# Which engine waits for the last store: moving the closing semaphore wait of an add-and-GELU kernel from SyncE to ScalarE

## The chip, the cores and the metric

The kernel runs on one core of a Trainium2 chip. The metric is the device time of one execution in microseconds (us), as a median over runs. The **span** is the time from the start of the first of the program's own instructions to the end of the last; it comes from the profile. All runs below are in the fast state. In some executions, of the kernel before too, the span is 0.4 to 0.9 us longer than in most; medians are little touched by that, and where less than 0.1 us matters I compare the time minus the span of one profiled execution, to which the store's landing adds nothing. Times are on record to 0.01 us, so the third digit of such a difference is no evidence; means over all runs of a kernel are given below as a check.

Engines: PE is TensorE, DVE is VectorE, ACT is ScalarE, POOL is GpSimd, SP is SyncE.

## The reference

```python
def setup_inputs():
    batch, dim = 1024, 4096
    # x, y: float32 of [batch, dim]
def reference(x, y):
    z = x + y
    return (0.5 * z * (1 + np.tanh(np.sqrt(2 / np.pi) * (z + 0.044715 * z ** 3)))).astype(np.float32)
```

## The kernel before

Loads, adds (mostly on GpSimd), two passes on ScalarE, two on VectorE, and three stores, all issued by SyncE. The change concerns none of it, only the end. Without `wait_late` the program closes as the run `undo_late` below shows: SyncE waits 11.5 us for its stores, the four other engines have a semaphore record at 119.1 to 119.2 us, GpSimd clears the semaphores at 119.4 us (a record of 95 ns), and all five have one at 119.7 us. I call these the kernel's own closing barriers, with the clearing between them. `wait_late`, run on the finished program, takes the last store out of that first wait, leaves its semaphore out of the clearing, and puts the wait for it at the very end, so that barriers and clearing run under the last store (in the kernel before from 111.75 to 112.49 us, with the last count of the store at 118.744 us):

```python
def wait_late(nc):
    body, end = (b.instructions for b in nc.main_func.blocks[1:3])
    last = [i for i in body if isinstance(i, mybir.InstDMACopy)][-1]
    (sem,) = [u.id for u in last.sync_info.on_update]
    # ... (cut: finds the closing wait, the clearing and its range)
    (its,) = [w for w in waits if w.id == sem]
    end[0] = mybir.InstDrain(   # waits for all but the last store
        name=all_done.name, engine=all_done.engine, debug=all_done.debug, is_reset_sema=False,
        sync_info=mybir.SyncInfo(on_wait=[w for w in waits if w.id != sem], on_update=[]),
    )
    # ... (cut: clears the semaphores on both sides of sem)
    end.append(
        mybir.InstEventSemaphore(
            name=clear.name, engine=mybir.EngineType.SP, debug=clear.debug,
            sync_info=mybir.SyncInfo(
                on_wait=[its],
                on_update=[
                    mybir.SyncUpdate(
                        sync_type="semaphore", id=sem, ant_name=its.ant_name,
                        update_mode="sem-sub-imm", update_value=its.wait_value,
                    )
                ],
            ),
        )
    )
```

## Time and profile before

| | before |
|---|---|
| time, median of 3 runs | 120.35 us (120.22 to 120.42) |
| span of the profiled run | 118.8 us |
| time of the profiled run minus its span | 120.44 − 118.778 = 1.66 us |
| busiest compute engine | VectorE, 62% of the span |
| DMA queue | 98.8% of 16 engines' time |

The kernel is bound by its transfers. The row to look at is the last: 1.66 us of the time lie outside the program's own instructions, and the change acts there. No page of the profile shows that part. The trace does, through its record of semaphore updates, which goes on after the program's last instruction (the prediction below shows the page's lines and reads them). Semaphore 2 is named by none of the 172 instructions that the trace holds, and yet it is updated 18 times from 112.727 to 120.227 us, in two groups of nine. I call a group a **barrier of the runtime**, since no line of the kernel makes it. The name is mine. The trace also has 223 updates of other semaphores, one of each, 0.26 to 0.87 us after the span's end, most of them between the two groups, and the texts call them resets. The 1.45 us from the span's end to the last update are what the prediction calls the postamble. A **hop** here is the time from one update of semaphore 2 to the next.

### The profile page before, as it was taken

The page shows a single profiled execution, that of the slowest core. Times are in us where ns is not written, and L with a number is a line of the kernel's source. Part 1 is how long each engine was busy: PE and PEld are TensorE (multiplying, and loading weights), DVE is VectorE, ACT ScalarE, POOL GpSimd, SP SyncE. Part 2 cuts the span into 40 slices and gives each one's busy share as a digit, 9 for nine tenths or more (in the row PEclk, how much of TensorE's full clock was granted, in tenths as well). Part 3 has the DMA queues.
Part 4 walks back from the last instruction along what each step waited for, and adds up shares of the span by engine and source line. Part 5 has one row for each costly group of instructions (what it writes and reads, how often), then busy time and mean ns, then how long its engine had stood idle before and what let it go on. Part 6 is the DMA issues. An engine that isn't in the chain of part 4 may idle for free.

```text
span 118.8 us, 172 instructions
## 1 busy us (share of the span) xinstructions
DVE 73.7 (62%) x35; ACT 61.0 (51%) x34; POOL 69.6 (59%) x19
## 2 busy tenths in 40 slices
DVE  0000000635799995739999968999994999990000
ACT  5000000063888965197698647888839779810000
POOL 0000000699996099999959999959999990000000
DMA  7989898989999898989899898998899889999996
GB/s 243 463 386 497 353 530 353 508 375 475 408 419 463 375 508 353 519 364 508 375 430 452 386 497 353 519 541 353 353 596 463 353 353 441 441 441 441 389 406 265
DMA packets 1584, 50.33 MB, mean 424 GB/s; under 512 B 176, under 2 KB 176, under 8 KB 176
## 3 DMA queue, kind: packets, MB, share of 16 engines
q1 hardware_dynamic: 1584, 50.33, 98.8%
HBM read 33.55 MB, written 16.78 MB: 424 GB/s over the span
## 4 chain that ended last, share of the span: by engine, by line
DMA 51%; POOL 26%; POOLq 4%; DVE 4%; DVEq 2%; ACT 2%; issue 0%; SPq 0%
DMA y<-in_y_dram 51%; POOL z L152 26%; POOLq L230 4%; DVE w L163 2%; DVEq L230 2%; DVE z L175 2%; ACT w L157 2%; SPq L128 0%; POOLq L152 0%
## 5 line engine op out<-in xcount | busy, mean ns | idle before, releaser
L152 POOL TENSOR_TENSOR z<-z,y 128x2048 f32<-128x2048 f32 x15 | 69.4, 4658 | 28.3 <-DMA y<-in_y_dram 28.3
L157 ACT ACTIVATE w<-z 128x2048 f32<-128x2048 f32 x16 | 30.1, 1882 | 37.7 <-DVE z L152 21.5
L163 DVE SCALAR_TENSOR_TENSOR w<-w,z 128x2048 f32<-128x2048 f32 x16 | 36.7, 2296 | 11.3 <-ACT w L157 11.1
L175 DVE TENSOR_TENSOR z<-w,z 128x2048 f32<-128x2048 f32 (+1 forms) x17 | 35.9, 2155 | 0.0
L168 ACT ACTIVATE w<-w 128x2048 f32<-128x2048 f32 x16 | 29.7, 1855 | 4.4 <-DVE w L163 4.3
L152 DVE TENSOR_TENSOR z<-z,y 128x2048 f32<-128x2048 f32 x1 | 2.3, 2291 | 20.5 <-DMA y<-in_y_dram 20.5
L215 ACT ACT_TABLE_LOAD x1 | 1.3, 1283 | 1.3 <-PEq L247 1.3
L214 DVE MEMSET one<- 128x1 f32 x1 | 0.1, 59 | 1.3 <-PEq L247 1.3
L247 POOL MEMSET const-float32-0.0<- 128x1 f32 x1 | 0.1, 99 | 0.2 <-issue 0.2
L215 ACT ACTIVATE one<-one 128x1 f32<-128x1 f32 x1 | 0.2, 203 | 0.0
L247 POOL MEMSET const-bfloat16-1.0<- 128x1 bf16 x1 | 0.1, 101 | 0.0
L247 POOL MEMSET const-uint8-127<- 128x1 uint8 x1 | 0.1, 101 | 0.0
L247 POOL MEMSET const-float32-1.0<- 128x1 f32 x1 | 0.1, 98 | 0.0
## 6 DMA issues: line engine op xcount, KB each, us to landing
z<-in_x_dram SPq DMA_DIRECT2D x4, 4096.0 KB, 31.4
y<-in_y_dram SPq DMA_DIRECT2D x4, 4096.0 KB, 22.2
out_dram<-z SPq DMA_DIRECT2D x1, 5120.0 KB, 15.8
out_dram<-z SPq DMA_DIRECT2D x1, 3072.0 KB, 11.9
out_dram<-z SPq DMA_DIRECT2D x1, 22.0
```

Source lines behind the costliest of these rows:

```text
L152: eng.tensor_add(out=zt[:, a:b], in0=zt[:, a:b], in1=yt[s][:, o : o + b - a])
L157: nc.scalar.activation(out=wt[c], in_=zt[:, a:b], func=act.Square, scale=root)
L163: nc.vector.scalar_tensor_tensor(out=wt[c], in0=wt[c], scalar=c1, in1=zt[:, a:b], op0=alu.add, op1=alu.mult)
L168: nc.scalar.activation(out=wt[c], in_=wt[c], func=act.Sigmoid)
L175: ins = nc.vector.tensor_mul(out=zt[:, a + o : a + o + n], in0=wt[c][:, o : o + n], in1=zt[:, a + o : a + o + n],)
L214: nc.vector.memset(one, 0.0)
L215: nc.scalar.activation(out=one, in_=one, func=act.Sigmoid)
L230: tc.compile()
L247: nc = _bacc.Bacc("TRN2", target_bir_lowering=False, num_devices=1)
```

## The change

ScalarE is idle at the end; the change lets it hold the last wait, so that SyncE, which issued every transfer, is free 6.3 us earlier.

```diff
     end.append(
         mybir.InstEventSemaphore(
-            name=clear.name, engine=mybir.EngineType.SP, debug=clear.debug,
+            name=clear.name, engine=mybir.EngineType.Activation, debug=clear.debug,
             sync_info=mybir.SyncInfo(
                 on_wait=[its],
```

## The prediction

> **What bounds the kernel now.** I read the views in this order: the page, to see which resource is full; the wait view of SyncE's queue, to see who holds the end of the program; the records of the line that closes the kernel; and last the trace's semaphore updates after the final instruction, which no page prints. From the page:
>
> ```profile
> span 118.8 us, 172 instructions
> DVE 73.7 (62%) x35; ACT 61.0 (51%) x34; POOL 69.6 (59%) x19
> DVE  0000000635799995739999968999994999990000
> ACT  5000000063888965197698647888839779810000
> POOL 0000000699996099999959999959999990000000
> DMA  7989898989999898989899898998899889999996
> q1 hardware_dynamic: 1584, 50.33, 98.8%
> DMA 51%; POOL 26%; POOLq 4%; DVE 4%; DVEq 2%; ACT 2%; issue 0%; SPq 0%
> ```
>
> The reader is to see that no compute engine passes 62% of the span, while the packets of the one DMA queue fill 98.8% of the 16 DMA engines' time. The kernel is bound by moving 50.33 MB. In the last four slices all three compute rows are 0 and the DMA row is still 9, 9, 9, 6: the program ends with a store alone. The chain adds to about 90%, since it is followed back from the last instruction of a compute engine (a VectorE multiply that ends at 106.84 us), so it says nothing of the last 12 us, which is where the change lies. For these I took one stretch, 107 to 119 us, with the busy time of each engine:
>
> ```profile
> 107.00:119.00 12.00, 0.00 (x0) 0.00 (x0) 0.00 (x0) 1.00 0.86 371
> ```
>
> Compute is 0.00 us, DMA 0.86 busy at 371 GB/s. Then the waits of SyncE's queue, the four lines that bear on the end:
>
> ```profile
> SPq L230 <- SPq L230: 6.3, 1, 6.3
> SPq L230 <- DMA out_dram<-z: 4.2, 1, 4.2
> SPq L230 <- PEq L230: 0.6, 2, 0.5
> ```
>
> The columns are total us, times, longest. (The fourth is the issue of the last store at 106.86 us, in the timeline.) The 4.2 us are the wait for the stores before the last. The 6.3 us are the wait that the change moves: SyncE passes the kernel's own closing barrier at 112.43 us, then sits until the last store's count is full. The view names SyncE itself as releaser only because SyncE's subtraction is the last update of that semaphore. The records of the closing line give the instruction behind it:
>
> ```profile
> L230 SPq EVENT_SEMAPHORE  x7: 17/28/4226, 107.2 to 118.8; - x7
> L230 ACTq EVENT_SEMAPHORE  x2: 17/17/17, 111.9 to 112.4; - x2
> ```
>
> SyncE's seventh starts at 118.8 us and ends the span; ScalarE's last is at 112.4 us, so ScalarE has been idle for 6.3 us by then.
>
> [...] the 6.3 us wait has a record of 17 ns. [...] The trace shows 16 increments, from 118.260 to 118.744 us, and the subtraction at 118.778. [...] The trace shows such hops, nine updates of semaphore 2 a barrier, 23 to 47 ns apart where nothing holds them; [...] the last update of semaphore 2 is at 120.227 us, 1.45 us after the span ends.
>
> **The change part by part.** *Removed and added:* one semaphore instruction leaves SyncE's stream and the same one, same wait, same subtraction, joins the end of ScalarE's. The comparison of the two programs' streams says "the same" for all five engines (it lists no semaphore instructions), so loads, compute and stores do not move: 118.744 us, when the count fills, stays. Bandwidth and bytes stay.
>
> *The wake-up:* in the closing barrier at 112.4 us both engines wait for one semaphore; SyncE's record starts at 112.430, ScalarE's at 112.434, both 17 ns. I take +0.004 us. What follows: from SyncE's record (118.761) to its update of the runtime's barrier (118.918) are 157 ns. For ScalarE I take the same, since from the barrier record to the next drain both engines need 91 to 92 ns at 111.9 us.
>
> *The place in the runtime's barrier:* this is the term that I think matters. In the barrier after the kernel four updates come at 112.727, 112.761, 112.966 and 113.010 us, all engines but SyncE; then nothing until SyncE's at 118.918; then 118.962, 119.001, 119.035, 119.082. [...] all others have already handed up, and only four hops down are left, 44 + 39 + 34 + 47 = 164 ns. If ScalarE comes last, the hops up from ScalarE to SyncE must still be made. The second barrier, which nothing holds, shows the steps: 119.870, .904, .942, .986, 120.010, .108, .146, .181, .227, that is 34, 38, 44, 24, 98, 38, 35, 46 ns. ScalarE's place I infer: in the kernel's own barrier SyncE answers 34 ns after the release, ScalarE 45, VectorE 57; 11 and 23 ns over SyncE, and the second place answers in 34 ns and the fourth in 44 against SyncE's 24, so ScalarE is second and VectorE fourth. From the second place: up 38 + 44 + 24 = 106 ns, then down 98 + 38 + 35 + 46 = 217, together 323 ns. The 98 is more than the 44 of before because the fourth engine has only just made its own update, and its next comes 122 ns after that one. So 323 − 164 = +159 ns. [...]
>
> *Sum:* 0.004 + 0.159 = +0.16 us, 0.14% of 120.35. The run that was profiled took 120.44 us against a span of 118.78; the 1.66 us between fit the 1.45 us of postamble plus a little at the start, so I count the postamble as timed. 120.35 + 0.16 = **120.5 us**.
>
> **The rivals.** *Nothing at all:* the wait only changes its owner, and the count fills at 118.744 either way. It holds if the timing stops at the span's end [...]. For it: the runs of one kernel spread from 120.22 to 120.42, more than my term. It would give 120.35. *A small gain:* SyncE owns the queue of all the stores; set free at 112.45 us, it might do some end-of-program work of its own under the last store, a part of the 157 ns. Against it: the four engines that were free before got no further than one barrier update each, and that barrier opens only when the last comes. At most some 0.1 us, so 120.25. *A slower sequencer:* ScalarE, after a 6 us wait, might need more than 157 ns to reach the barrier. VectorE and TensorE are slower than SyncE in the closing barrier, ScalarE only by 4 to 11 ns. TensorE's answer, 57 ns over SyncE's, is the worst there, so at most +0.06, 120.57. *A different place:* if ScalarE were first, one hop of 34 ns more (+0.19); if fourth, only 24 + (98 − 44) = 78 ns (+0.08). Every place is later than SyncE's.
>
> **Range and chances.** The mechanism gives +0.08 to +0.25; the runs' spread is 0.1 to each side, and the changed kernel may be timed on another day or chip, for which I add 0.1 below. That gives 120.25 to 120.75. A change of 2% is 2.4 us; the whole postamble is 1.45 us and the wake-up 0.03, so no part that is touched is that large. I give faster 0.005 and slower 0.01 for what I have not thought of.
>
> **What will show it.** In the changed profile SyncE has six of the closing line's semaphore instructions, the last at 112.4 us; ScalarE has three, the last at about 118.8; the 6.3 us line leaves SyncE's waits. The span stays within its noise, some 0.1 us, of 118.8. In the updates of semaphore 2 only one engine comes before the long pause, not four, eight come after it, and from the first of these to the last are about 0.32 us, not 0.16. The prediction is wrong if the second to fifth updates come before the store has landed, if ScalarE needs far longer to its first update, or if the time falls although the tail grows.

Cut are passages that rest on no trace of this case (the second condition of "nothing at all", that ScalarE were as good a place as SyncE, went with their words), and a sentence that the trace contradicts in part: all of the 0.159 us were to lie on the path because the resets and the second barrier come after the first, but the first reset comes 43 ns before that barrier's last update (261 against 304 ns after the span's end). That the whole 0.159 us delay what follows is seen in the result: the second barrier starts 1251 ns after the span's end in place of 1092. The "23 to 47 ns" between updates leave out the hop behind SyncE's update, the fifth of the nine, which takes 98 ns, as the prediction says further on. No trace names the engine that makes an update of semaphore 2; the places in the order are inference from the times.

## The result and the profile after

The changed kernel took 120.35 us (median of 6 runs, 120.29 to 120.43), the kernel before 120.41 us (6 runs, the first three and those of the same rounds, 120.22 to 120.84). The ratio is 0.9992, with a 95% interval of 0.9975 to 1.0008: the same. (The ratios are from the fast runs of the same rounds; they are not quite the ratios of the medians.)

From the page of the changed kernel, the span, the DMA row and the queue:

```profile
span 118.7 us, 172 instructions
...
DMA  8989898989999898989999898998899889999896
...
q1 hardware_dynamic: 1584, 50.33, 98.8%
```

Nothing moved there. The waits of SyncE's queue (total us, times, longest):

```profile
SPq L230 <- DMA out_dram<-z: 4.3, 1, 4.3
...
SPq L230 <- PEq L230: 0.6, 2, 0.5
```

The line of 6.3 us is gone. The records of the closing line (count, shortest, median and longest in ns, first and last start in us):

```profile
L230 SPq EVENT_SEMAPHORE  x6: 17/28/4270, 107.1 to 112.4; - x6
...
L230 ACTq EVENT_SEMAPHORE  x3: 17/17/17, 111.9 to 118.7; - x3
```

SyncE has six, the last at 112.4 us, ScalarE three, the last at 118.7: the wait changed hands as meant. Now the updates of semaphore 2 after the program, in ns from the end of the span, from the two traces (a table of mine, not a page):

```
                     first barrier                                    second barrier
before   -6051 -6017 -5812 -5768 |  140  184  223  257  304    1092 1126 1164 1208 1232 1330 1368 1403 1449
after    -6024 |  140  178  222  246  344  383  417  464       1251 1286 1324 1368 1391 1490 1528 1679 1726
```

The bar stands for the landing of the store. Three things are to be seen. First, after the landing the first barrier takes 464 − 140 = 324 ns, against 304 − 140 = 164: eight updates, so seven hops, in place of five updates and four hops, as the prediction counts and at the size it gives. Second, one hop of the second barrier has grown: 1528 to 1679 is 151 ns where before had 1368 to 1403, 35 ns. No one predicted that; by the order that the five holders below show, the place is ScalarE's. Third, the last update comes 277 ns later, and yet the time minus the span did not grow: 120.35 − 118.702 = 1.65 us, against 1.66. So 0.29 us were given back after that update, or the time does not contain this barrier at all. That is what the experiments had to settle.

### The profile page after: what moved, and what is told of

The parts are those of the page before. It is cut to its first block, busy times and chain, and to the rows that moved or that the text cites. A ratio compares the mean times of both kernels' runs of the same rounds, so it can differ in the third digit from the quotient of the medians.

```text
span 118.7 us, 172 instructions
## 1 busy us (share of the span) xinstructions
DVE 73.7 (62%) x35; ACT 61.0 (51%) x34; POOL 69.6 (59%) x19
## 4 chain that ended last, share of the span: by engine, by line
DMA 51%; POOL 26%; POOLq 4%; DVE 4%; DVEq 2%; ACT 2%; issue 0%; SPq 0%
DMA y<-in_y_dram 51%; POOL z L152 26%; POOLq L230 4%; DVE w L163 2%; DVEq L230 2%; DVE z L175 2%; ACT w L157 2%; SPq L128 0%; POOLq L152 0%
```

## The experiments

Each kernel was timed over five rounds against the kernel before on the same chip (the four sets of experiments ran on four chips); the time minus the span is that of its profiled execution. All gave correct results.

### Who holds the wait

Theory A: the time ends with the span, and the runtime's barriers are not in it. Theory B: they are. Theory C: it ends with the last engine's first update in them. The edit is the engine's name alone:

```diff
-            name=clear.name, engine=mybir.EngineType.SP, debug=clear.debug,
+            name=clear.name, engine=mybir.EngineType.PE, debug=clear.debug,
```

and likewise `DVE`, `Pool`, `Activation` (the changed kernel once more), and `SP` (the kernel before against itself).

> The kernel before, against itself: how fine the comparison is, and whether its tail repeats. Theory A (the time ends with the span, the runtime's barrier is not in it): ratio 1.000, time minus span 1.66 us as in the first profile of before. Theory B (the runtime's barrier is in the time): the same. Both: four updates of semaphore 2 before the store has landed, five after it, 0.16 us from the first of the five to the last.

> The changed kernel again. Both theories expect one update of semaphore 2 before the landing, eight after it, 0.32 us from the first to the last, as in its first profile. Theory A: time minus span stays 1.65 us, ratio to before 1.000. Theory B: time minus span is 0.16 us more, 1.82, ratio 1.0013.

> TensorE, not ScalarE, waits last. If TensorE is the first place of the runtime's barrier, no update of semaphore 2 comes before the landing and nine after it, 34 + 38 + 44 + 24 + 98 + 38 + 35 + 47 = 0.36 us from the first to the last. Theory A (time ends with the span): time minus span 1.65 us, ratio 1.000 to 1.0005. Theory B (barrier timed): time minus span 1.85 us, ratio 1.0016. Theory C (the time ends with the last engine's own first barrier update): TensorE needs 286 ns from its record to that update where SyncE needs 157, so time minus span about 1.75 us.

> VectorE waits last. If it is the fourth place: three updates of semaphore 2 before the landing, six after it, 24 + 98 + 38 + 35 + 47 = 0.24 us from the first to the last. Theory A: time minus span 1.65 us, ratio 1.000. Theory B: 1.73 us, ratio 1.0007.

> GpSimd waits last. If it is the third place: two updates of semaphore 2 before the landing, seven after it, 44 + 24 + 98 + 38 + 35 + 47 = 0.29 us from the first to the last. GpSimd's own way to its first update is long (in before 578 ns from its last record, SyncE 157). Theory A (time ends with the span): time minus span 1.65 us, ratio 1.000. Theory B (the runtime's barrier is timed): 0.12 us more for the hops and 0.42 for the way, so 2.2 us, ratio 1.0045. Theory C (the time ends with the last engine's first barrier update): 2.08 us, ratio 1.0035.

That the wait moved is seen in the closing line's records, of the kernels where TensorE, VectorE and GpSimd hold it:

```profile
L230 PEldq EVENT_SEMAPHORE  x3: 51/51/51, 111.8 to 118.7; - x3
```

```profile
L230 DVEq EVENT_SEMAPHORE  x3: 21/21/21, 111.8 to 118.7; - x3
```

```profile
L230 POOLq EVENT_SEMAPHORE  x5: 17/17/17, 111.8 to 118.7; - x5
```

| holder | updates before the landing | span's end to its first update, ns | from there to the barrier's last, ns | time − span, us | median us (before) | ratio, 95% interval |
|---|---|---|---|---|---|---|
| SyncE, again | 4 | 141 | 164 | 1.67 | 120.38 (120.42) | 0.9998 (0.9985 to 1.0010) |
| VectorE | 3 | 182 | 242 | 1.79 | 120.50 (120.42) | 1.0007 (0.9994 to 1.0020) |
| GpSimd | 2 | 562 | 285 | 2.21 | 120.97 (120.41) | 1.0053 (1.0037 to 1.0070) |
| ScalarE, again | 1 | 140 | 324 | 1.65 | 120.35 (120.42) | 1.0003 (0.9990 to 1.0016) |
| TensorE | 0 | 279 | 358 | 1.99 | 120.70 (120.42) | 1.0024 (1.0010 to 1.0038) |

The second column gives the order of the barrier: TensorE, ScalarE, GpSimd, VectorE, SyncE. The fourth column is the hops that are left, up to SyncE's update and down from it, and comes out at the expected numbers within a few ns. Theory A falls: with the span unchanged the time grows with the third and fourth columns. For TensorE they are 139 and 194 ns over the kernel before, 1.66 + 0.33 = 1.99 us, as measured; for VectorE 1.66 + 0.04 + 0.08 = 1.78, measured 1.79; for GpSimd 1.66 + 0.42 + 0.12 = 2.20, measured 2.21. Theory C falls with TensorE, where it expects 1.75 (1.79 if its own 286 and 157 ns are added rightly) and 1.99 is measured, and with GpSimd, 2.08 against 2.21. What the expectations under theory B missed for TensorE and VectorE was the slower way to the first update, which they had only for GpSimd.

So the runtime's barriers are timed and my term is real. ScalarE is the one row that does not obey: by the same sum it should be at 1.66 + 0.16 = 1.82, and it stands at 1.65, twice. Something of 0.17 us is won on ScalarE.

### Two controls inside the program

One kernel hands the full count to and fro between SyncE and ScalarE before the last subtraction, the other has no late wait (the first edit is shortened here to its loop).

```diff
+    hops = 16
+    for k in range(hops + 1):   # engine: ScalarE for odd k, SyncE for even k
+        # waits for its.wait_value + k; adds 1, or subtracts all when k == hops
```

```diff
-    wait_late(nc)
```

> Control inside the program: after the last store's count is full, SyncE and ScalarE hand it to each other 16 times, then SyncE subtracts. Nothing else differs. Hops of 35 to 60 ns as in the kernel's own barriers: span longer by 0.6 to 1.0 us. Theories A and B both: time longer by the same 0.6 to 1.0 us, ratio 1.005 to 1.008, time minus span stays 1.66 us. If the time did not follow, the end of the program's own instructions would not be what is timed either.

> The late wait taken out whole: SyncE waits for all stores before the kernel's closing barriers, which in before ran under the last store from 111.57 to 112.49 us. Now they follow the landing: span longer by 0.7 to 1.0 us. Theory A: time longer by as much, ratio 1.006 to 1.008, time minus span 1.65 us. Theory B: all engines come to the runtime's barrier at about one time, so the first barrier takes up to 0.36 us after the span in place of 0.16 and more until GpSimd's update, time minus span 1.9 to 2.2 us.

The relay took 121.27 us, ratio 1.0077 (1.0060 to 1.0094). Its 16 hand-overs take 645 ns from the first to the last record, 40 ns each, so the span grew as expected. But its time minus span was 1.90 us and not 1.66, against what I had expected of both theories. Part of this theory B should have foreseen: ScalarE passes on its last count 40 ns before SyncE's last record, so here too it comes late to the runtime's barrier, and the hops from its place are left after its first update, 325 ns in all. The rest is new: ScalarE, which does nothing new after the landing but pass a count on, made its first update of the runtime's barrier 597 ns after its last record (540 ns after the span's end), where the changed kernel took 157. A stall of 0.44 us sits on ScalarE again, at another place than in the changed kernel. And in this kernel the time ends 0.11 us before the last update of semaphore 2, counted from the span's start; in the kernels above that leave ScalarE's stream alone it ends 0.21 to 0.22 us after it, in the changed kernel 0.08 us before it.

Without the late wait the kernel took 121.87 us, ratio 1.0120 (1.0107 to 1.0133). Its waits on SyncE's queue show the store's whole flight:

```profile
SPq L230 <- DMA out_dram<-z: 11.5, 1, 11.5
...
SPq L230 <- PEq L230: 0.6, 2, 0.4
```

The span, 119.8 us, is 1.0 us longer, as expected of either theory, and the time minus span is 2.12 us, which theory B alone expects (theory A's ratio, 1.006 to 1.008, is missed as well): all engines enter the runtime's barrier together, TensorE first at 234 ns and GpSimd late, and the barrier ends 759 ns after the span.

### Where the stall sits

What the changed kernel and the relay share is that ScalarE's instruction stream is longer, by one and by eight. (In the changed kernel SyncE's is one shorter too, but so it is with TensorE, VectorE and GpSimd as holders, which show no stall of this kind.) Theory F: at a fixed count of instructions in ScalarE's stream there is a stall. In the kernel before it would lie behind ScalarE's last update, where no record shows it, at the very end of the timed part, with nothing to hide it. One more instruction would move it ahead of that update, where ScalarE waits for other engines anyway and part of it is hidden. Theory G: what helps is that ScalarE holds the wait. To tell them apart, empty drains are added to ScalarE's stream while it is idle at the start, with SyncE or ScalarE as the holder, and to VectorE's as a control (one edit for all, shortened):

```diff
+def pad(nc, engine, count):
+    body = nc.main_func.blocks[1].instructions
+    at = next(k for k, i in enumerate(body) if i.engine == engine and isinstance(i, (mybir.InstActivation, mybir.InstMemset)))
+    debug = body[at].debug
+    for k in range(count):
+        body.insert(at + 1 + k, mybir.InstDrain(
+            name=f"I-{900000 + k}", engine=engine, debug=debug, is_reset_sema=False,
+            sync_info=mybir.SyncInfo(on_wait=[], on_update=[])))
...
     wait_late(nc)
+    pad(nc, mybir.EngineType.Activation, 1)     # 16; 16 and the wait on ScalarE; DVE, 16; 2
```

> SyncE waits last as in before; one empty drain is added to ScalarE's stream, in its idle time at 3 us. So far the time was the last update of semaphore 2 plus 0.21 to 0.22 us in every kernel whose ScalarE stream is untouched, and that update minus 0.08 where ScalarE has one instruction more. Theory F (a stall sits at a fixed count of instructions in ScalarE's stream, in before after its last update; one more instruction moves it to before that update): the hop to ScalarE in the second barrier's way down takes 0.15 us in place of 0.035, the time is the last update minus 0.08, time minus span 1.49 us, ratio 0.9985. Theory G (what helps is that ScalarE, not SyncE, holds the wait): time minus span 1.66, ratio 1.000.

> SyncE waits last; 16 empty drains in ScalarE's stream at 3 us. Theory F: the stall comes before the long wait for the last store and costs nothing: hops as in before, time the last update minus 0.11 us, time minus span 1.33 us, ratio 0.9973. Theory G: 1.66, ratio 1.000.

> ScalarE waits last, and its stream has 16 empty drains at 3 us. Theory F: hops of the changed kernel without its slow one, so the last update 1.61 us after the span; the time is that minus 0.11, so 1.50 us after the span, ratio 0.9987. The 0.16 us of the barrier that I predicted stand between this and the kernel with SyncE and the same 16 drains. Theory G: as the changed kernel, 1.65.

> Control: SyncE waits last, the 16 empty drains stand in VectorE's stream at 1.4 us, while it waits for the first load. Theory F with the stall in ScalarE's stream alone: as before, time minus span 1.66 us, ratio 1.000. If any stream will do, time minus span 1.33.

The drains are in the trace, in ScalarE's idle start (the kernel with 16 and SyncE as holder):

```profile
L229 ACTq DRAIN  x16: 8/8/1359, 1.4 to 3.3; - x16
```

| holder | drains | time − span, us, expected by F | measured | median us (before 120.41) | ratio, 95% interval |
|---|---|---|---|---|---|
| SyncE | 1, ScalarE | 1.49 | 1.490 | 120.19 | 0.9988 (0.9960 to 1.0016) |
| SyncE | 16, ScalarE | 1.33 | 1.327 | 120.35 | 0.9987 (0.9965 to 1.0010) |
| ScalarE | 16, ScalarE | 1.50 | 1.484 | 120.56 | 1.0003 (0.9983 to 1.0023) |
| SyncE | 16, VectorE | 1.66 | 1.686 | 121.17 | 1.0060 (1.0039 to 1.0082) |

Theory F's numbers come out in all four, the last within 0.03; theory G's in none of the first three. The other runs bear the single executions out: the record gives each run's span to 0.1 us, and the mean of time minus span over the six runs of each of the four is 1.485, 1.325, 1.47 and 1.67 us, over the five of the changed kernel run again 1.65, and for the kernel before 1.66 to 1.67 on each of the four chips.

The updates of the second barrier, in ns from the end of the span, and the end of the time on the same scale (again a table of mine):

```
                             T    A    P    V    S    V    P    A    T | time
before                    1092 1126 1164 1208 1232 1330 1368 1403 1449 | 1662
SyncE, 1 on ScalarE       1092 1126 1165 1208 1231 1331 1369 1539 1586 | 1490
SyncE, 16 on ScalarE      1093 1127 1165 1208 1232 1331 1369 1403 1450 | 1327
ScalarE, 16 on ScalarE    1250 1285 1323 1367 1390 1489 1527 1561 1608 | 1484
SyncE, 16 on VectorE      1094 1128 1167 1211 1234 1333 1371 1405 1452 | 1686
```

The letters are the places in the order (TensorE, ScalarE, GpSimd, VectorE, SyncE, and down again; the order down is inferred). With one drain the slow hop appears at ScalarE's place of the second barrier, 1369 to 1539 ns, though SyncE holds the wait; with 16 no hop is slow and the time ends 0.12 us before the last update.

The times do not follow as cleanly, because with 16 drains the span grew: 118.9 to 119.2 us over the runs with the drains on ScalarE, whichever engine held the wait, and 119.4 to 119.8 with the drains on VectorE, where I had expected no change at all. The queues of the DMA view show what came in, first of the kernel with 16 drains on ScalarE and SyncE as holder, then of that with 16 on VectorE:

```profile
q1 hardware_dynamic: 1584, 50.33, 98.5%
q14 instruction: 1, 0.01, 0.0%
```

```profile
q1 hardware_dynamic: 1584, 50.33, 98.2%
q14 instruction: 1, 0.01, 0.0%
```

A packet of the instruction queue, 8192 bytes by the trace, starts among the stores at 98.6 us and at 118.4 us; the kernel with 16 drains and ScalarE as holder has one too, at 98.7 us. The last of the store's 16 counts comes 296 ns after the fifteenth in the first kernel, 754 ns in the second and 289 ns in the third, against 100 ns in the kernel before and 26 to 171 ns in the other ten profiled runs, in which no such packet comes before the landing. That this packet holds up the one count is argued from its place and not tested alone; why it costs more with the drains on VectorE is open. Nor would it be the only cause of a late landing: the profiled run of the relay has none before its landing, and its span was 119.9 us where most of that kernel's runs had 119.3 to 119.4.

### A version that beats both

To have no stall at the end and no packet beside the stores, the stall must lie between the two barriers, where ScalarE waits for the first update of the second (1.09 us after the span). Two drains should put it there.

> SyncE waits last, two empty drains in ScalarE's stream. The aim is a version that beats both kernels. With 16 drains the stall cost nothing after the span, but a packet of the instruction queue came to lie beside the stores and the span grew by 0.2 us or more; with one drain the span stayed and 0.16 us of the stall were left. Theory F: two drains put the stall between ScalarE's resets, [...] and its first update in the second barrier, due at 1.13 us, where it is hidden but for at most 0.05 us: time minus span 1.33 to 1.38 us, span as in before, no packet of the instruction queue in the span, ratio 0.9970 to 0.9976. Theory F', where the stall's place moves by more than one instruction for each drain: 1.49 or 1.66.

That ScalarE makes resets of its own, and when they end, was the author's estimate: no record says which engine makes which of the updates between the barriers.

It took 120.07 us against 120.36, ratio 0.9976 (0.9957 to 0.9995), with the time minus span at 1.324 us (1.32 as the mean of its six runs), just under the 1.33 to 1.38 expected, and with no slow hop in its barriers. The landing of the profiled run was a late one (the median run's span was 118.7 us), but its queue line has no second one below it:

```profile
span 119.1 us, 174 instructions
...
q1 hardware_dynamic: 1584, 50.33, 98.8%
```

So 0.3 us are won, 0.2% of the time, by two instructions that do nothing. Its interval lies below 1, but narrowly, and the gain is a quarter of a per cent; the 0.34 us less between span and time are the firmer evidence. That the stall now lies between the two barriers fits these numbers, but no record shows it there.

## Why the prediction was right or wrong

**What bounds the kernel, and that no part touched is large**: right; transfers and span are unchanged, and the time moved by less than 0.1%.

**The wake-up and the 157 ns to ScalarE's first update**: right. ScalarE's record starts 21 ns after the count is full, where SyncE's started 17 ns after it, the 0.004 us of the sum. It starts at 118.685 us and its update comes at 118.842, 157 ns on.

**The place in the runtime's barrier, +0.159 us**: right in mechanism, order and size. The five holders show the order, the hops take 324 ns against 323 worked out, and with the stall out of the way the same swap of holders costs 1.484 − 1.327 = 0.157 us of time.

**Counting the postamble as timed**: right, though the changed kernel alone seemed to say otherwise. TensorE, VectorE and GpSimd as holders settle it.

**The sum, 120.35 + 0.004 + 0.159 = 120.5 us**: this step failed, by a term that it lacked. Of the part "Removed and added" it took only the instruction's own wait and subtraction; it held that nothing else moves, since the comparison of the streams said "the same". But that comparison leaves semaphore instructions out, and ScalarE's stream had become one longer. The runs split the time minus span into three terms, from the kernel with SyncE and 16 drains, 1.327 us:

- before: 1.327 + 0.335 that vanish with the 16 drains, the stall that theory F puts at the end of ScalarE's stream = 1.662 us;
- after: 1.327 + 0.157 for the barrier + 0.163 for what is left of the stall when it stands one instruction earlier (the one-drain kernel, 1.490 − 1.327) = 1.647 us, measured 1.648.

So +0.157 and −0.335 + 0.163 = −0.172 cancel to −0.015 us. The change moved the time by nothing because two effects of one size met, not because it touched nothing. (By the means over all runs the terms are 0.34, 0.145 and 0.16 us and the sum for the changed kernel 1.63, measured 1.65; so the terms hold to some 0.02 us, and that they meet to 1 ns above is chance.) The mechanism's own +0.08 to +0.25 us, that is 120.43 to 120.60, missed; the range of 120.25 to 120.75 held the 120.35 only by the margins that I had added for the runs' spread and the other chip. That is luck. The prediction named the sign that would refute its sum, "if the time falls although the tail grows"; the first comparison showed something near it: the tail grew by 0.28 us and the time did not rise.

**The rivals**: "nothing at all" forecast the number and is wrong as a reason. The small gain from an early SyncE is not seen: in the runs of both holders the first update after the landing comes 140 ns after the span's end, and SyncE's early arrival opens nothing.

**Open**: what the stall is. Its place depends on the number of instructions in ScalarE's stream, and a packet of the instruction queue appears in the span when that stream, or VectorE's, is 16 longer. That the two have one cause is not shown: no such packet is seen near the stall in the kernel before, the changed one or the one-drain kernel, in the relay one starts 0.45 us after ScalarE's late update, and no run measured the distance to the next stall. Open too is what the time's two ends are to the nanosecond: in kernels without the stall it is 0.11 to 0.13 us shorter than from the first record to the last update of semaphore 2.

## What to carry to other kernels

The runtime's closing barrier was part of the time here, and the engine that came to it last set how many hops were left: SyncE cost least (164 ns of hops, 1.66 to 1.67 us from span to time), and GpSimd most (285 ns of hops and a first update 562 ns after the span, 0.55 us over SyncE). One empty drain on ScalarE (the median record of sixteen is 8 ns) took 0.17 us off the time minus the span (1.66 to 1.49 us), and two took 0.34 us (1.32 us), so a change of a few tenths of a microsecond must be tested with empty instructions as a control before its mechanism is believed. And a result of "the same" can be two terms that cancel: compare the time minus the span, and the records after the last instruction, before calling a cost hidden.
